# Pick weights laid out by groups of four blocks, and their DMAs issued by SyncE

## The chip, the cores and the metric

One core of one Trainium2 chip runs the program. The metric is device time in microseconds (us), the median of several executions. A profile is one execution, recorded by the hardware; its instructions' times are counted from the span's start.

The engines: TensorE (PE) multiplies matrices, VectorE (DVE), ScalarE (ACT) and GpSimd (POOL) work on tiles, SyncE (SP) does nothing here but issue DMAs. DMAs can also be issued by ScalarE and by GpSimd. SyncE's DMAs are queue q1 of the profile, ScalarE's q10, GpSimd's indirect ones q0; sixteen DMA engines serve all of them.

## The reference

One layer of a decoder trunk, for 512 prompt tokens and 64 sample tokens of width 2048. What matters here is its last part, a mixture of 16384 single-neuron experts (PEER):

```python
q = (xb @ w_q).reshape(PEER_BLOCK, PEER_HEADS, 2, HALF_DIM)
sc = jnp.einsum('thpk,pnk->thpn', q, sub_keys)
v1, i1 = lax.top_k(sc[:, :, 0], PEER_TOPK)
v2, i2 = lax.top_k(sc[:, :, 1], PEER_TOPK)
...                                   # the best 16 of the 256 sums, for each of 8 heads
g = jax.nn.softmax(top, axis=-1)
act = jax.nn.gelu(jnp.einsum('td,thkd->thk', xb, expert_u[eidx])) * g
return jnp.einsum('thk,thkd->td', act, expert_v[eidx])
```

Before it come the modulation (adaLN), an input projection, two recurrent and convolutional head groups and an output projection; after it a last RMSNorm. Everything is in float32.

## The kernel before

**Stages.** Up to about 950 us: modulation, projections, scans. To about 1200 us: the queries and most of the choice of experts. Then two dense stages of about 1000 us each, which the change touches.

The 16384 experts are 128 blocks of 128. The 80 most often picked blocks are computed densely for all 512 prompt tokens; picks that fall in the other 48, and all picks of the sample tokens, are done by gathering single rows of u and v (1 MB per gather of 128 rows), with VectorE multiplying and adding.

- **The u stage** (`for n in range(NU2)`, 160 half blocks): `load(n)` (L892) fetches half a block of u (`raw<-ut`, 512 KB) with SyncE, `conv(n)` splits it into a high part on ScalarE (`xhi`, L908) and a low part on GpSimd (`xlo`, L909), and `u_half` multiplies both with the tokens (`pu`, L1405, three products of float32r for one of float32). After two halves ScalarE applies the gelu (`act`, L1408) and stores the block's activations (`actd<-act`, L1409).
- **The pick weights.** Meanwhile, once the choice is sorted, TensorE makes for each token a 128 x 80 table with the softmax weight of the picked expert, by products of one-hot rows (`gbank`, L1605; the operands come from VectorE, L1591, and ScalarE, L1599). ScalarE copies it out into a tile for 32 tokens (`stg`, L1612), two of which exist. When 32 tokens are done, four stores (`gd<-stg`, L1617, 320 KB each, 20 blocks) are put on a list, `puts`, and `put(2)` issues two of them in each following half.
- **The v stage** (80 steps of 4 columns): `load` fetches pieces of v (`raw<-v`, L897, 256 KB each, four to a step), `conv` splits them, and `v_column` (`pv`, L1425, 12 matmuls a column) adds up the products with the weighted activations. These come in tiles of four blocks (`SG = 4`, 20 tiles): `load_weights` (L1356, `gsb<-gd`, four quarters of 256 KB) and `load_acts` (L1363, `actr<-actd`, two halves of 512 KB) fetch them, `weigh` (L1368, VectorE) multiplies them in place, `halve` splits the product (`ahi`, L1375, ScalarE; `alo`, L1379, VectorE). There is one buffer for gsb and one for actr, so the next tile's loads wait for the product before.

**What sets the order.** From the last query on, the order on every engine is the one in which the code is written (`manual_schedule`), so on each engine's queue an instruction waits behind those written before it. Waits between engines are semaphores that the framework places; every DMA issued by SyncE or ScalarE gets one of eight completion semaphores in turn (DMAHW0 to DMAHW7 in the built program), and waits until the DMA that had it before is complete.

The loads are written ahead of use by `ahead(l, c)`: load up to piece l, split up to piece c. In the u stage there are three raw buffers (`n % 3`), in the v stage five:

```python
ahead(n + 3, n + 2)        # u stage, at the start of half n
...
ahead(n + 3, n + 3)        # v stage, at the start of a step
ahead(n + 8, n + 3)
```

At `E0`, 14 halves before the u stage ends, the remaining stores are issued, the memory of the choice is given free, and the first two weight and activation tiles are loaded into it.

Of the kernel before, what the change touches and what calls it, by code (L numbers as in the profile page):

```python
# [5 lines left out]
F32 = mybir.dt.float32  # L6
# [25 lines left out]
L = 80  # L32
SG = 4
# [3 lines left out]
TC = 32  # L37
NCH = NA // TC
# [43 lines left out]
def build(ctx, tc, A, O, dbg=None):  # L82
    nc = tc.nc
# [6 lines left out]
    dr = ctx.enter_context(tc.tile_pool(name="dr", bufs=1, space=DRAM))  # L90
# [339 lines left out]
    def project(src, nm):  # L430
        his, los = stream_w(src, nm)
        p = pp.tile([128, 2, 512], F32, name=f"pp_{nm}", tag="pp")
        mm3([p[:, 0, :HT], p[:, 1, :HT]], his, los, movs)
        return p
# [183 lines left out]
    for k in range(KD):  # L618
        if k < 2:
            out_half(k, 1)  # L620
            p = p_out[k]
        else:
            p = project(A["w_out"][k], f"o{k}")
# [31 lines left out]
    for q in range(4):  # L655
        modulate(x1, R, None, 3, 4 * q, 4, "h2")
        mm3(pq0, *w_q, movs, range(4 * q, 4 * q + 4))
        t = adap.tile([128, 4, 512], F32, name=f"h2s{q}", tag="wa")
# [41 lines left out]
    identr = rt.tile([128, 128], F32R, name="identr")  # L700
    V.tensor_copy(identr, ident)
    pickd = dr.tile([NA, 2 * NPK], F32, name="pickd")
    gd = dr.tile([NCH, 128, L, TC], F32, name="gd")
    actd = dr.tile([L // SG, 128, SG, NA], F32, name="actd")
    accd = dr.tile([NA, D], F32, name="accd")
    accs = dr.tile([128, D], F32, name="accs")
# [170 lines left out]
    raws, parts, gsb, ahl, acts, pools = {}, {}, {}, {}, {}, {}  # L877
# [6 lines left out]
    def load(n):  # L884
        if n >= len(stream):
            return
        s = stream[n]
        k = n % 3 if n < NU2 + 2 else (n - NU2 - 2) % 5
        pool, b = (ws, 2) if k < 2 else (wx, 1) if k == 2 else (pools["vx"], 2)
        raw = pool.tile([128, 8, 128], F32, name=f"raw{n}", tag="wraw", bufs=b)  # L890
        if s[0] == "U":
            nc.sync.dma_start(raw, A["ut"][bass.ds(block(s[1]), 1), :, 8 * s[2]:8 * s[2] + 8, :].rearrange("o p k c -> p (o k) c"))  # L892
        else:
            _, i, q = s
            r2 = raw.rearrange("p (a k) c -> p a (k c)", a=2)
            for a in range(2):
                nc.sync.dma_start(r2[:, a, :], v3[bass.ds(block(i + a), 1), :, q * VC:(q + 1) * VC].rearrange("o p c -> p (o c)"))  # L897
        raws[n] = raw
# [15 lines left out]
    def ahead(l, c):  # L914
        while at["l"] <= min(l, len(stream) - 1):
            load(at["l"])
            at["l"] += 1
        while at["c"] <= min(c, len(stream) - 1):
            conv(at["c"])
            at["c"] += 1  # L920
# [430 lines left out]
    def load_weights(sg, q):  # L1351

        if q == 0:
            gsb[sg] = ep.tile([128, NCH, SG * TC], F32, name=f"gsb{sg}", tag="gsb", bufs=1)
        c = slice(q * NCH // GP, (q + 1) * NCH // GP)
        nc.scalar.dma_start(gsb[sg][:, c, :], gd[c, :, sg * SG:(sg + 1) * SG, :].rearrange("c p i t -> p c (i t)"))  # L1356

    def load_acts(sg, q):

        if q == 0:  # L1360
            acts[sg] = ep.tile([128, SG, NA], F32, name=f"actr{sg}", tag="actr", bufs=1)
        i = slice(q * SG // AP_, (q + 1) * SG // AP_)
        nc.scalar.dma_start(acts[sg][:, i, :], actd[sg][:, i, :])  # L1363

    def weigh(sg):

# [141 lines left out]
    it, stg, pair, puts = [], {}, {}, []  # L1508
# [99 lines left out]
    def g_out(b, pg):  # L1608
        c, b0 = divmod(b, TC // 4)
        if b0 == 0:  # L1610
            stg[c] = pools["rg"].tile([128, L, TC], F32, name=f"stg{c}", tag="stg", bufs=2)
        S.activation(stg[c][:, :, b0 * 4:b0 * 4 + 4].rearrange("p i t -> p t i"),  # L1612
                     pg[:, :4 * L].rearrange("p (t i) -> p t i", t=4), AF.Copy)
        if b0 == TC // 4 - 1:
            full = stg.pop(c)
            for q in range(0, L, L // 4):
                puts.append(lambda q=q: nc.scalar.dma_start(gd[c][:, q:q + L // 4, :], full[:, q:q + L // 4, :]))  # L1617

    def put(n):
        for f in puts[:n]:  # L1620
            f()
        del puts[:n]
# [20 lines left out]
    for n in range(NU2):  # L1643
        _, i, c = stream[n]
        if n == 0:
            sample_twice()
        if n == 1:
            sample_rows()
        ahead(n + 3, n + 2)
        spare += PIECE if R1 is None else PIECE_G  # L1650
        if R1 is not None:
            put(2)
            g_one(n)
            if not gk:
                g_start()
            elif gm[0] < min(upto(n), gm[1] + PAIRS - 1):
                g_pair(gm[0])
                gm[0] += 2
                spare -= 2.2
            while gm[2] < gm[3]:  # L1660
                g_scale(gm[2])
                gm[2] += 1
            gm[3], gm[4] = gm[4], gm[0]

        even, waits = R2 is not None, False
        while spare > 0 and R2 is None:
            cost = next(steps1 if R1 is None else steps2, "end")
            if cost == "end":
                if R1 is None:
                    R1 = n  # L1670
                else:
                    R2 = n
                break
            if cost is None:
                waits = True
                break
            spare -= cost
        if not even:
            if since is None and ready[0]:
                since = n  # L1680
            if since is not None and n == since + 1:
                fetch_to(RB - 1)
            if since is not None and n > since + 2:
                due_g += RATE[R1 is not None] + (0.7 if waits and spare > 4.5 else 0.0)
            g0 = gu[0]
            gather_to(due_g, ready[0])
            if gu[0] == ready[0] and sorted_[0]:
                fetch_to(gu[0] + 1, ready[0])
            due_g = min(due_g, gu[0] + 1.0)
            spare -= 2.4 * (gu[0] - g0)  # L1690
            if waits:
                spare = min(spare, 3.0)
            G0 = gu[0]
        else:
            gather_to(G0 + (NU + EARLY_V - G0) * (n - R2) // (NU2 - 1 - R2))
        if n == E0:
            assert not pair and not stg
            put(len(puts))
            p2.close()
            epx = ctx.enter_context(ExitStack())  # L1700
            ep = epx.enter_context(tc.tile_pool(name="ep", bufs=1))
        u_half(n, i, c)
        for sg, o in ((0, 1), (1, 7)):
            d = n - E0 - o
            if 0 <= d < 2:
                load_weights(sg, 2 * d)
                load_weights(sg, 2 * d + 1)
            if 2 <= d < 4:
                load_acts(sg, d - 2)
            if d == 5 - sg:  # L1710
                weigh(sg)
            if d == 6 - sg:
                halve(sg, 0)
            if d == 7 - sg:
                halve(sg, 1)
# [39 lines left out]
    for m in range(M):  # L1755
        gi, q, bl, first, final = steps[m]
        n = NU2 + 2 * m
# [6 lines left out]
        for kq in range(KD // VQ):  # L1764
# [7 lines left out]
            if (m, kq) in tplan:  # L1772
                t = len(fin["tok"])
# [168 lines left out]
```

## Time and profile before

| | us |
|---|---|
| median of 3 runs | 3207.52 |
| lowest, highest | 3200.43, 3209.41 |
| the profiled execution | 3200.89 |
| its span, first to last instruction | 3199.1 |
| TensorE busy in it | 3067.4 |
| VectorE, GpSimd, ScalarE busy | 2167.9, 1701.2, 1044.3 |

The issues of the DMAs in question, from the page (count, size of each):

```profile
raw<-ut SPq DMA_DIRECT2D x160, 512.0 KB
raw<-v SPq DMA_DIRECT2D x320, 256.0 KB
actd<-act ACTq DMA_DIRECT2D x80, 256.0 KB
gd<-stg ACTq DMA_DIRECT2D x64, 320.0 KB
gsb<-gd ACTq DMA_DIRECT2D x80, 256.0 KB
actr<-actd ACTq DMA_DIRECT2D x40, 512.0 KB
```

How to read what follows: in a view by stretches, each row gives start and end, the length, the busy time and number of instructions of each engine, the granted TensorE clock (1 is full), the mean busy share of the 16 DMA engines (slightly over 1 is possible at a stretch's edges), and GB/s. Rows of a queue give packets, MB and the time that they took as a share of 16 engines over the stretch. Rows of waits give who waited for whom, the total, how often, and the longest. In the chain of waits each row is a start, a length, and what it was. A `q` after an engine (SPq, ACTq) is its queue of DMA issues.

### The profile page before, as it was taken

Reading aid. Unit: us, or ns where it says so; the run is one execution under the profiler, and the core shown is the slowest. Engines: PE = TensorE matmul, PEld = TensorE weight load, DVE = VectorE, ACT = ScalarE, POOL = GpSimd, SP = SyncE. Lnnn points to the kernel's source line nnn. Section 1 sums busy time; section 2 is a strip of 40 time slices with the busy share of each in tenths; the row PEclk is TensorE's granted clock in tenths of the full one; section 3 lists DMA queues with packets and bytes.
Section 4 is the critical chain, followed back from the end, with each engine's and each line's share of the span. In section 5 each row is a group of like instructions: output and inputs, shape, how many; then the busy total and the mean of one; then the engine's idle time right before and its main releaser. Section 6 shows DMA issues by size and latency. Waiting matters only on the chain.

```text
span 3199.1 us, 46649 instructions
## 1 busy us (share of the span) xinstructions
PE 3067.4 (96%) x17239; PEld 2606.4 (81%) x17239; DVE 2167.9 (68%) x3267; ACT 1044.3 (33%) x1640; POOL 1701.2 (53%) x1001
## 2 busy tenths in 40 slices
PE   6999999999989999999999999998999999899997
PEld 2788888899979998887888788886888878688776
DVE  3455521142245898977898999856777888788755
ACT  3244311122232232232655555542322222121222
POOL 2233333344334235666666666656777677668742
PEclk9999999999989999999999999999999999999998
DMA  9744566633332227899889898989999999899964
GB/s 394 275 139 139 174 218 209 204 121 135 134 117 90 68 82 250 309 314 398 339 309 405 345 410 356 389 288 376 400 386 385 395 329 347 322 399 350 374 206 159
DMA packets 297067, 882.84 MB, mean 276 GB/s; under 512 B 37590, under 2 KB 79446, under 8 KB 245366
## 3 DMA queue, kind: packets, MB, share of 16 engines
q1 hardware_dynamic: 160608, 380.39, 33.8%
q0 software_dynamic: 66336, 413.41, 32.5%
q10 hardware_dynamic: 69888, 86.00, 7.6%
q8 instruction: 136, 2.23, 0.3%
q14 instruction: 99, 0.81, 0.1%
HBM read 879.89 MB, written 66.81 MB: 296 GB/s over the span
## 4 chain that ended last, share of the span: by engine, by line
PE 73%; DMA 11%; POOL 5%; issue 5%; DVE 4%; ACT 1%; SPq 1%; ACTq 0%; POOLq 0%; DVEq 0%
PE pu L1405 20%; PE pv L1425 18%; PE pp_o L140 6%; DMA raw<-v 4%; DMA gsb<-gd 4%; PE pp_c L140 3%; PE pp_s L140 3%; PE qa L140 3%; PE pp_b L140 3%; PE qb L140 3%; POOL xlo L909 3%; PE ada L190 2%; PE pp_x L140 2%; PE pp_y L140 2%; PE gbank L1605 2%
## 5 line engine op out<-in xcount | busy, mean ns | idle before, releaser
L909 POOL TENSOR_TENSOR xlo<-raw,xhi 128x1024 fp32r<-128x1024 f32 x320 | 777.9, 2442 | 420.7 <-ACT xhi L908 408.5
L908 ACT ACTIVATE xhi<-raw 128x1024 fp32r<-128x1024 f32 x320 | 337.5, 1060 | 880.0 <-DMA raw<-v 221.4
L1263 DVE SCALAR_TENSOR_TENSOR u<-u,hT 128x2048 f32<-128x2048 f32 x223 | 503.6, 2283 | 107.4 <-DMA u<-u,rows 88.6
L1290 DVE SCALAR_TENSOR_TENSOR accB<-v,dots,accB 128x2048 f32<-128x2048 f32 x211 | 496.5, 2353 | 106.3 <-DMA v<-v,rows 100.7
L1425 PE MATMUL pv<-ahi,xhi 128*128 128x512 f32 x1280 | 512.0, 400 | 23.8 <-ACT xhi L908 15.7
L1425 PE MATMUL pv<-ahi,xlo 128*128 128x512 f32 x1280 | 510.0, 398 | 11.4 <-POOL xlo L909 11.4
L1405 PE MATMUL pu<-hhi,xhi 128*128 128x512 f32 x1280 | 513.9, 402 | 0.0
L1425 PE MATMUL pv<-alo,xhi 128*128 128x512 f32 x1280 | 506.5, 396 | 0.0
L1405 PE MATMUL pu<-hhi,xlo 128*128 128x512 f32 x1280 | 502.3, 392 | 0.8 <-POOL xlo L909 0.8
L1405 PE MATMUL pu<-hlo,xhi 128*128 128x512 f32 x1280 | 502.9, 393 | 0.0
L1235 POOL DMA_INDIRECT u<-u,rows x223 | 224.3, 1006 | 209.5 <-DVE u L1263 145.0
L1425 PEld LDWEIGHTS pv<-ahi,xhi 128*128 128x128 f32 x1280 | 243.9, 191 | 81.1 <-ACT xhi L908 17.4
L1425 PEld LDWEIGHTS pv<-ahi,xlo 128*128 128x128 f32 x1280 | 243.5, 190 | 72.6 <-POOL xlo L909 16.1
L1425 PEld LDWEIGHTS pv<-alo,xhi 128*128 128x128 f32 x1280 | 244.0, 191 | 55.2
L1405 PEld LDWEIGHTS pu<-hhi,xlo 128*128 128x128 f32 x1280 | 240.8, 188 | 55.6 <-POOL xlo L909 1.5
L1235 POOL DMA_INDIRECT v<-v,rows x223 | 253.5, 1137 | 57.9 <-issue 38.7
L1405 PEld LDWEIGHTS pu<-hhi,xhi 128*128 128x128 f32 x1280 | 241.2, 188 | 49.6 <-issue 0.9
L1405 PEld LDWEIGHTS pu<-hlo,xhi 128*128 128x128 f32 x1280 | 241.2, 188 | 48.3
L1599 ACT ACTIVATE op<-op,it 128x128 f32<-128x128 f32 x512 | 155.4, 389 | 36.7 <-DVE op L1591 34.7
L1605 PEld LDWEIGHTS gbank<-wr,op 128*128 128x128 f32 x1024 | 132.8, 191 | 22.9 <-ACT stg L1612 13.9
L1447 DVE TENSOR_TENSOR acc<-acc,pv 128x512 f32<-128x512 f32 x144 | 97.1, 682 | 67.1 <-PE pv L1425 66.3
L129 POOL TENSOR_TENSOR wlo_o<-raw_o,whi_o 128x1024 fp32r<-128x1024 f32 x32 | 77.5, 2423 | 119.9 <-ACT whi_o L127 119.9
(498 smaller groups left out, 5458.9 us busy)
## 6 DMA issues: line engine op xcount, KB each, us to landing
wa<-w_ada SPq DMA_DIRECT2D x96, 1024.0 KB
raw<-ut SPq DMA_DIRECT2D x160, 512.0 KB
raw<-v SPq DMA_DIRECT2D x320, 256.0 KB
actd<-act ACTq DMA_DIRECT2D x80, 256.0 KB
gd<-stg ACTq DMA_DIRECT2D x64, 320.0 KB
gsb<-gd ACTq DMA_DIRECT2D x80, 256.0 KB
actr<-actd ACTq DMA_DIRECT2D x40, 512.0 KB
raw_o<-w_out SPq DMA_DIRECT2D x32, 512.0 KB
```

Of the source, the lines that this page charges most:

```text
L129: lo_engine(share).tensor_sub(lo, raw, r32(hi))
L140: PE.matmul(o, st, mv[pick](k), start=first, stop=last)
L908: S.activation(hi, raw, AF.Copy)
L909: G.tensor_sub(lo, raw, r32(hi))
L1235: G.indirect_dma_start(out=out, out_offset=None, in_=src, in_offset=bass.IndirectOffsetOnAxis(ap=idx, axis=0), bounds_check=NE * 128 - 1, ...
L1263: V.scalar_tensor_tensor(r, r, 1.0, st["h"], op0=ALU.mult, op1=ALU.mult, accum_out=dots[i][:, j:j + 1])
L1290: V.scalar_tensor_tensor(st["a"], r, dots[i][:, j:j + 1], st["a"], op0=ALU.mult, op1=ALU.add)
L1405: PE.matmul(pu, st[:, kk, :], movA[mv](k), start=k == 0 and a == 0, stop=k == KD - 1 and a == 2)
L1425: PE.matmul(pv, st, mv, start=first and j == 0 and a == 0, stop=last and not end and j == SG - 1 and a == 2)
L1447: V.tensor_add(ak, ak, pv)
L1599: S.activation(ops[:, j0 + j, :], ops[:, j0 + j, :], AF.Copy, scale=it[2][:, b * 4 + j:b * 4 + j + 1])
L1605: PE.matmul(pg[:, j * L:(j + 1) * L], ops[:, j0 + j, :], wr[:, j0 + j, :], start=True, stop=True)
```

## The change

Three edits. **The layout of `gd`**, the pick weights in memory, goes from chunks of 32 tokens outermost, `[chunk, partition, block, token]`, to groups of four blocks outermost, `[group, partition, chunk, block of the group, token]`. A quarter of a gsb tile is then 4 x 4 x 32 numbers in a row for each partition, where it was four runs of 4 x 32; a store of 20 blocks is five runs of 4 x 32 for each partition, where it was one of 20 x 32. The bytes and the number of DMAs stay. **The issuer** of the stores of pick weights and of the loads of pick weights and activations becomes SyncE. ScalarE keeps the stores of activations. **Raw u** is written up to five half blocks ahead: a second call follows the first, with nothing more to split.

```diff
-    gd = dr.tile([NCH, 128, L, TC], F32, name="gd")
+    gd = dr.tile([L // SG, 128, NCH, SG, TC], F32, name="gd")
...
-        nc.scalar.dma_start(gsb[sg][:, c, :], gd[c, :, sg * SG:(sg + 1) * SG, :].rearrange("c p i t -> p c (i t)"))
+        nc.sync.dma_start(gsb[sg][:, c, :], gd[sg][:, c].rearrange("p c i t -> p c (i t)"))
...
-        nc.scalar.dma_start(acts[sg][:, i, :], actd[sg][:, i, :])
+        nc.sync.dma_start(acts[sg][:, i, :], actd[sg][:, i, :])
...
-                puts.append(lambda q=q: nc.scalar.dma_start(gd[c][:, q:q + L // 4, :], full[:, q:q + L // 4, :]))
+                puts.append(lambda q=q: nc.sync.dma_start(
+                    gd[q // SG:(q + L // 4) // SG, :, c].rearrange("s p i t -> p s (i t)"),
+                    full[:, q:q + L // 4, :].rearrange("p (s i) t -> p s (i t)", i=SG)))
...
         ahead(n + 3, n + 2)
+        ahead(n + 5, n + 2)
```

What this does to the order on the engines, at the places of which the prediction speaks (numbers are part of the names; `x2` stands for two such rows).

ScalarE in the v stage, before: the splits of raw v, with the loads of weights and activations between them.

```order
L908 ACTIVATE xhi_21459<-raw_21279 128x1024
L1356 DMA gsb_21536<-gd 128x4x128
L908 ACTIVATE xhi_21551<-raw_21288 128x1024
L908 ACTIVATE xhi_21555<-raw_21375 128x1024
L1375 ACTIVATE ahi_21577<-actr_21315 128x2048
L1356 DMA gsb_21536<-gd 128x4x128 x3
L908 ACTIVATE xhi_21641<-raw_21384 128x1024
L908 ACTIVATE xhi_21645<-raw_21463 128x1024
L1363 DMA actr_21690<-actd 128x1024 x2
L908 ACTIVATE xhi_21742<-raw_21472 128x1024
```

With the change the six DMA rows are gone from ScalarE here, and the splits follow each other. They stand on SyncE, here for the next tile, behind the raw v loads of the same step (TENSOR_LOAD and ISA read and use the block's number):

```order
L897 DMA raw_21943<-v 128x512
L881 TENSOR_LOAD blk
L897 ISA
L897 DMA raw_21943<-v 128x512
L1356 DMA gsb_21911<-gd 128x512 x3
L881 TENSOR_LOAD blk
L897 ISA
L897 DMA raw_22024<-v 128x512
```

SyncE had nothing but raw loads there before; a load of the next step now waits behind the three quarters.

SyncE in the u stage, with the change: the stores of one chunk of 32 tokens between raw u loads.

```order
L892 DMA raw_15365<-ut 128x1024
L1617 DMA gd<-stg_14986 128x5x128 x2
L881 TENSOR_LOAD blk
L892 ISA
L892 DMA raw_15430<-ut 128x1024
L1617 DMA gd<-stg_14986 128x5x128 x2
L881 TENSOR_LOAD blk
L892 ISA
L892 DMA raw_15483<-ut 128x1024
```

Before, only the raw rows stood here, and the four stores stood on ScalarE behind splits of raw u.

## The prediction

> **What bounds the kernel now.** I read the page first: busy shares, DMA row, queues, chain.
>
> ```profile
> PE 3067.4 (96%) x17239; PEld 2606.4 (81%) x17239; DVE 2167.9 (68%) x3267; ACT 1044.3 (33%) x1640; POOL 1701.2 (53%) x1001
> DMA  9744566633332227899889898989999999899964
> q1 hardware_dynamic: 160608, 380.39, 33.8%
> q0 software_dynamic: 66336, 413.41, 32.5%
> q10 hardware_dynamic: 69888, 86.00, 7.6%
> PE 73%; DMA 11%; POOL 5%; issue 5%; DVE 4%; ACT 1%; SPq 1%; ACTq 0%; POOLq 0%; DVEq 0%
> PE pu L1405 20%; PE pv L1425 18%; PE pp_o L140 6%; DMA raw<-v 4%; DMA gsb<-gd 4%; PE pp_c L140 3%; PE pp_s L140 3%; PE qa L140 3%; PE pp_b L140 3%; PE qb L140 3%; POOL xlo L909 3%; PE ada L190 2%; PE pp_x L140 2%; PE pp_y L140 2%; PE gbank L1605 2%
> ```
>
> TensorE is the bound almost everywhere. The DMA engines are nearly full from slice 15 on, the two dense stages, and only there do DMAs (raw v, and the pick weights gsb) enter the chain. Which queue is whose follows from sizes: q0 the gathers, q1 SyncE's, q10 ScalarE's. Next the view by stretches, for what TensorE loses.
>
> ```profile
> core 0: us, PE busy (x) PEld busy (x) DVE busy (x) ACT busy (x) POOL busy (x), PEclk, DMA share, GB/s
> 2200.00:3040.00 840.00, 804.81 (x3417) 648.33 (x3416) 672.84 (x379) 193.64 (x185) 598.31 (x362) 0.98 0.97 368
> 2280.00:2520.00 240.00, 240.00 (x1043) 195.40 (x1042) 184.71 (x111) 54.48 (x49) 170.53 (x104) 1.00 1.01 388
> 2200.00:2240.00 40.00, 30.09 (x120) 23.18 (x119) 25.49 (x12) 11.91 (x14) 25.37 (x16) 0.87 0.93 363
> 2560.00:2600.00 40.00, 35.10 (x133) 27.06 (x132) 29.56 (x18) 8.15 (x7) 26.15 (x15) 0.87 0.95 358
> 2760.00:2800.00 40.00, 28.45 (x103) 21.48 (x104) 34.78 (x16) 9.13 (x9) 29.43 (x18) 0.83 0.96 341
> 2960.00:3000.00 40.00, 33.30 (x135) 25.86 (x134) 29.93 (x18) 8.89 (x8) 23.92 (x15) 0.95 1.00 371
> ```
>
> The undisturbed stretch has 1043 matmuls in 240 us: 0.230 us each, 174 in 40 us. The v stage, 840 us, would hold 3651 at that pace and has 3417: 234 missing, **54 us**. The four short stretches lack 54, 41, 71 and 39, together 205, or 47 of the 54. Their clock is below 1: a stall also buys some microseconds at half clock. The chain of waits, in order of time, shows what each stall hangs on.
>
> ```profile
> 2533.78 30.96 DMA gsb<-gd
> 2564.86 0.33 SPq L897
> 2565.70 11.13 DMA raw<-v
> 2578.07 2.39 POOL xlo L909
> 2580.51 136.63 PE pv L1425 x580
> ...
> 2718.14 29.98 DMA gsb<-gd
> ...
> 2826.14 28.09 DMA gsb<-gd
> ```
>
> A quarter of a gsb tile (256 KB) takes 28 to 31 us; when it lands, SyncE issues a raw v load, 11 us later that lands, is split, and TensorE resumes. Yet raw v and gsb share no data. In the built program each load issued by SyncE or ScalarE waits for the completion semaphore of an earlier one, eight semaphores serving both queues in turn; so a slow gsb holds a raw load back. The waits of SyncE's and ScalarE's queues from 2240 to 3040 us say how much:
>
> ```profile
> SPq L897 <- POOL xlo L909: 187.7, 72, 7.2
> SPq L897 <- DMA raw<-v: 161.0, 55, 13.1
> SPq L897 <- DMA gsb<-gd: 105.3, 13, 18.4
> SPq L897 <- DMA actr<-actd: 30.6, 13, 4.5
> ...
> ACT xhi L908 <- DMA raw<-v: 212.5, 38, 16.3
> ...
> ACT xhi L908 <- DMA actr<-actd: 31.9, 5, 8.6
> ACT xhi L908 <- DVE actr L1368: 29.0, 3, 11.3
> ACT xhi L908 <- DMA gsb<-gd: 25.8, 3, 8.6
> ```
>
> The last three rows are ScalarE standing in front of its own gsb and actr issues while the next split (L908) is queued behind.
>
> **The change part by part.** *Layout of gd.* A quarter tile was 512 runs of 512 B and becomes 128 runs of 2 KB; a store was 128 runs of 2560 B and becomes 640 of 512 B. Prices, each from a stretch in which one size makes up nearly all of a queue (gsb on q10 from 2624.7 to 2635.3; raw v on q1 from 2242 to 2264; gd stores on q10 from 1755.9 to 1762):
>
> ```profile
> q10 hardware_dynamic: 2112, 1.05, 35.9%
> ...
> q1 hardware_dynamic: 1710, 3.11, 38.1%
> ...
> q10 hardware_dynamic: 98, 0.25, 10.2%
> ```
>
> 35.9% of 16 engines x 10.6 us over 2112 packets is 28.8 ns for 512 B; likewise 78 ns for 2 KB and 102 ns for 2560 B. Loads: 80 x 512 x 28.8 ns / 16 = 74 us of all engines' time become 80 x 128 x 78 / 16 = 50, a saving of 24, some 21 of it in the v stage. Stores: 64 x 128 x 102 / 16 = 52 us become 64 x 640 x 28.8 / 16 = 74, a cost of 22 in the u stage. No row shows 512 B written to memory; from below it is the read's 28.8 ns, from above a whole packet of the old store, 102 ns, which would cost 209 us; I take the read's, since 2 KB read and 2560 B written cost alike per byte (0.038 and 0.040 ns).
>
> The Trainium skill ("DMA: Bandwidth & Descriptors", Specifications) puts the smallest transfer at line rate at 512 B, by which neither side of the new layout would change the engines' time and both terms, -21 and +22, would be nothing. The rows disagree: 512 B in 28.8 ns is a third fewer bytes per ns than 2 KB in 78, so the measurement decides.
>
> *What that is worth in the v stage.* Its DMA work is 0.97 x 840 = 815 us and falls to 794; TensorE needs 3417 x 0.230 = 786. So the stage cannot end earlier than about 794 by DMA: at most 46 us of gain, unless the gathers fill less of it. From below: if the engines stay idle for the 25 us that they are now, the gain is the 21 us saved. Between lies the order of issue. All streams now stand in one queue, complete in nearly the order of issue, and a semaphore used eight issues earlier is then mostly free, so the 105 + 31 us of SyncE's waits on gsb and actr should shrink to waits on plain backlog. I take **33 us**: the stage at 807, a DMA share of 0.984, between the 0.97 of the whole and the 1.01 that the undisturbed stretch held while TensorE lost nothing.
>
> *ScalarE rid of 184 issues.* From the rows of these tiles:
>
> ```profile
> L1356 ACTq DMA_DIRECT2D gsb<-gd x80: 367/408/12334, 2153.0 to 3009.8; - x80
> L1617 ACTq DMA_DIRECT2D gd<-stg x64: 326/442/1412, 1564.6 to 2138.0; - x64
> ```
>
> About 0.4 us each, 75 us, on an engine that is busy 33%: nothing by itself (its idle time hides them; were it the bound, 75 us); its 87 us of waits above are part of the 33. SyncE takes the issues over and does no other work. But now SyncE stands before a gsb load until the product before it (DVE, L1368) is done, with raw loads behind; those have 3 steps of 48 matmuls, 11 us each, before they are split, and the longest such wait on ScalarE was 11.3: nothing (without that lead, up to 11 us a tile).
>
> *The u stage.* Stores enter SyncE's queue between raw u loads. Raw n+5 reuses the buffer that split n+2 has just left, so issuing it five ahead puts it before the stores, and it still goes out when the buffer is free, as before: nothing, where three ahead would have left it behind two stores. What is new is one ring.
>
> ```profile
> 1560.00:2120.00 560.00, 552.66 (x2865) 465.96 (x2864) 506.82 (x636) 323.05 (x706) 350.20 (x237) 1.00 0.92 367
> 1680.00:1800.00 120.00, 114.26 (x588) 94.49 (x586) 107.87 (x147) 66.41 (x145) 73.47 (x51) 1.00 1.00 411
> ...
> ACT xhi L908 <- DMA raw<-ut: 28.7, 15, 4.8
> PEld gbank L1605 <- ACT stg L1612: 12.6, 13, 3.6
> ```
>
> (The last two: waits from 1560 to 1800.) The engines have room on average: 0.92 x 560 + 22 = 537 of 560. But in the first 240 us the split already waits for raw u, 15 times, and TensorE then waits for ScalarE behind it. Two stores are 16 shares per engine of 5 x 28.8 ns; with a gather's 8 KB (at most 0.33 us, by q0's row of the page: 32.5% of 16 x 3199 us over 413.41 MB) between each two, they occupy the ring for 7.6 us, by which the next raw u may land later. Lower end nothing; upper end 7.6 us in each of the 240 / 36 = 6.7 chunks of that window, 51 us (36 us: 16 chunks from 1565 to 2138). I take one shift, **7 us**: raw u is released by GpSimd's split, not by TensorE, so a TensorE that has fallen 7 us behind finds the next loads in time. The move to v, at 2200, is in the 33.
>
> **Sum:** -33 + 7 = -26. The profiled execution took 3200.89 us (span 3199.1), 6.6 below the median of 3207.52 whose runs spread over 9; against the median, 3207.5 - 26 = **3181 us**.
>
> **Rivals.** (1) *All stalls go*: 54 back, no price in u: 3153. For it: four stalls hang on the same wait. Against: 794 us of DMA work. (2) *DMA time is the bound*: 21 saved in v, 22 paid in u, and idle engines as now: about 3207. For it: share 1.00 in both stages' worst stretches. Against: 45 us idle in u. (3) *Slower, by stores ahead of raw u*: in SyncE's ring the delay returns with every chunk, 51 - 33 = +18, 3225. It decides once the delays in u add up to more than 33 us, that is, when over 4 of the 16 chunks cost 7.6 us each. For it: raw u has no slack there now; against: one shift makes slack. (4) *Slower, by the share of the queue*: in v three queues become two; from 2240 on SyncE's one ring must carry what took two, and with a gather always waiting, each 2 KB of weights or raw v costs 0.33 + 0.08 us. It decides if raw v then lands as late as it did behind gsb: nothing is gained in v, u's 7 stay: 3214. Against it: the gathers wait for row buffers. The Trainium skill ("DMA: Bandwidth & Descriptors", Queues, rings and completion order) has each engine go round the queues packet by packet, by which moving two streams into one queue costs them a turn, as in (4); the gsb quarters of 28 to 31 us on a queue of their own agree with waiting for turns.
>
> The change does what it says: the built order has all 184 DMAs on SyncE.
>
> **Chances.** Forecast 0.52 (its own range 3165 to 3198), rival 1 0.14, rival 2 0.16, rival 3 0.11, rival 4 0.07. What a measurement here tells from no change is 0.3%, 9.6 us: faster below 3198, slower above 3217. Faster: 0.52 x 0.95 + 0.14 + a fifth of rival 2 = 0.66; same: the rest of these and half of rival 4, 0.19; slower: rival 3 and half of rival 4, 0.15. Range 3148 to 3215: it leaves out the lowest of rival 1 and most of rival 3.
>
> **What would show it.** Right: matmuls from 2200 to 3040 up to some 3560, no gsb in the chain, SyncE's waits on gsb under 30 us, ScalarE's on actr and gsb gone; u stage longer by under 10 us. Wrong: raw<-ut waits of the split far above 40 us and the v stage starting 20 us later or more (rival 3); raw<-v waits above 212 us with as many matmuls lost (rival 4); q1's 512 B packets well above 29 ns (the store's price); DMA share at 1.00 throughout v with 230 matmuls missing still (rival 2).

## The result, and the profile after

The changed kernel takes **3250.01 us** (median of 4 runs, 3246.95 to 3259.81), the kernel before 3208.47 beside it: a ratio of 1.0136, with a 95% interval of 1.011 to 1.0161. It is slower by 1.4%, where 0.8% faster was forecast, and outside the range.

The profiled execution of the changed kernel took 3248.33 us. Its page, with the rows that answer to those shown of before:

```profile
PE 3075.5 (95%) x17239; PEld 2615.7 (81%) x17239; DVE 2160.2 (67%) x3267; ACT 1041.4 (32%) x1640; POOL 1705.6 (53%) x1001
q1 hardware_dynamic: 219872, 443.31, 39.3%
q10 hardware_dynamic: 12672, 23.07, 1.9%
PE 69%; DMA 17%; DVE 5%; issue 4%; POOL 3%; ACT 1%; SPq 0%; POOLq 0%; DVEq 0%; ACTq 0%
PE pu L1405 19%; PE pv L1425 16%; DMA raw<-v 7%; PE pp_o L140 6%; DMA raw<-ut 6%; PE pp_c L140 3%; PE pp_s L140 3%; PE qa L140 3%; PE pp_b L140 3%; PE qb L140 3%; PE pp_x L140 2%; PE pp_y L140 2%; PE ada L190 2%; PE gbank L1605 2%; POOL xlo L909 2%
```

The gsb load is gone from the chain's list, as forecast, but DMA has 17% of the chain (11% before), and raw u, which was not in the list at all, has 6%. In what follows the u stage is the time from the first `pu` product to the first `pv` product, the v stage from the first to the last `pv` product, both from the trace. Before, they are 1025.4 and 960.6 us; in the changed kernel 1072.0 and 961.2. So **u lost 47 us and v gained nothing.** The view by stretches, of the changed kernel and then of the kernel before (the last row of each is the same piece of v, counted from 30 us ahead of its first product):

```profile
1560.00:2120.00 560.00, 514.97 (x2615) 435.00 (x2614) 480.25 (x611) 291.90 (x650) 324.52 (x221) 0.95 0.90 344
2200.00:3040.00 840.00, 812.29 (x3467) 656.78 (x3466) 656.22 (x374) 197.56 (x189) 600.70 (x361) 0.98 0.96 371
2231.00:3111.00 880.00, 844.76 (x3593) 682.28 (x3592) 694.98 (x397) 206.25 (x196) 620.46 (x373) 0.98 0.94 363
```

```profile
2184.00:3064.00 880.00, 844.01 (x3586) 679.98 (x3585) 708.60 (x398) 205.16 (x195) 616.93 (x371) 0.98 0.96 363
```

While the pick weights are stored, TensorE issues 2615 matmuls where it issued 2865, and the DMA engines are less busy than before (0.90 against 0.92): on the average of this stretch they are not the bound. In v the DMA share falls from 0.96 to 0.94, some 18 us of DMA work (16 by the packets' own times) where 21 was forecast, and the matmuls stay about the same (3593 against 3586).

**Where u went.** Waits from 1560 to 2160 us in the changed kernel, and then the same four in the kernel before:

```profile
POOL xlo L909 <- ACT xhi L908: 197.1, 57, 13.3
ACT xhi L908 <- DMA raw<-ut: 83.1, 13, 14.9
PEld gbank L1605 <- ACT stg L1612: 48.6, 9, 14.0
PE gbank L1605 <- ACT stg L1612: 45.0, 8, 13.5
```

```profile
POOL xlo L909 <- ACT xhi L908: 38.0, 13, 8.5
ACT xhi L908 <- DMA raw<-ut: 32.6, 17, 4.8
PEld gbank L1605 <- ACT stg L1612: 13.1, 14, 3.6
PE gbank L1605 <- ACT stg L1612: 7.1, 9, 3.2
```

TensorE does not wait for raw u. It waits for ScalarE to copy out the bank of the one-hot products (`stg`, L1612), and ScalarE stands ahead of that copy at the split of a half block that TensorE needs only two halves later. One such place in ScalarE's timeline (start, length, what, and in brackets the idle time before it):

```profile
1718.84 0.33 ACTq L1409 DMA_DIRECT2D actd<-act  x1
1731.88 1.06 ACT L908 ACTIVATE xhi<-raw 128x1024 fp32r<-128x1024 f32 x1 [13.07 <-DMA raw<-ut]
1732.84 0.70 ACT L1612 ACTIVATE stg<-gbank 128x320 f32<-128x320 f32 x1
```

That raw u load had been issued at 1704.55, behind two stores, as SyncE's timeline shows:

```profile
1697.27 1.04 SPq L1617 DMA_DIRECT2D gd<-stg  x2
1704.55 0.59 SPq L892 DMA_DIRECT2D raw<-ut  x1
1705.19 19.25 SPq L1617 DMA_DIRECT2D gd<-stg  x2
```

The chain of waits has it, with others like it:

```profile
1580.82 26.19 DMA raw<-ut
...
1704.55 27.25 DMA raw<-ut
...
1911.12 24.95 DMA raw<-ut
```

Why a 512 KB load took 27 us is told by the queues from 1704.5 to 1728 (packets, MB, share of 16 engines):

```profile
q0 software_dynamic: 1183, 8.64, 87.7%
q1 hardware_dynamic: 1187, 0.60, 8.4%
```

SyncE's queue moved 1187 packets, nearly all of 512 B (1170 by size in the trace, 27 ns each), and the gathers' queue 1183 (1055 of 8 KB, 309 ns each): about one for one. The order agrees: up to 1727 us, 1197 times a 512 B packet begins in the 6 ns before an 8 KB packet ends, where some 290 would be chance, and there is no such peak of 512 B packets behind one another. **Every piece of 512 B (a run of bytes in a row) took a turn of its own, against 8 KB of a gather.** The two stores of 1697.27 are 80 pieces on each engine, 80 x (0.309 + 0.027) = 27 us, and the raw load queued behind them comes after that: none of its 4 KB packets moves before 1728. By the Trainium skill ("DMA: Bandwidth & Descriptors", Queues, rings and completion order) an engine drains a packet of typically 9 to 17 descriptors before it turns to the next queue; by estimate 80 pieces would then be at most 9 turns, some 5 us by the durations above if a gather's turn is one 8 KB. The rows disagree for these stores.

**Where v went.** Waits at the product of weights and activations (L1368) in the stretch 2231 to 3111 of the changed kernel:

```profile
DVE actr L1368 <- DMA raw<-v: 45.4, 6, 16.0
DVE actr L1368 <- DMA actr<-actd: 31.3, 5, 11.8
DVE actr L1368 <- issue: 9.6, 2, 6.2
```

VectorE stands 86 us before this product; before it was 13 us in the same piece of v. The product does not read raw v; its operands now come in one queue with raw v. From issue to landing actr takes 18.2 us at the median (9.5 before), gsb 10.7 (16.6 before). ScalarE's splits wait less for raw v (144 us, 221 before): part of the stall has moved from the raw loads to the weighted activations.

### The profile page after: what moved, and what is told of

The parts are those of the page before. It is cut to its first block, busy times and chain, and to the rows that moved or that the text cites. A ratio compares the mean times of both kernels' runs of the same rounds, so it can differ in the third digit from the quotient of the medians.

```text
span 3246.5 us, 46716 instructions
## 1 busy us (share of the span) xinstructions
PE 3075.5 (95%) x17239; PEld 2615.7 (81%) x17239; DVE 2160.2 (67%) x3267; ACT 1041.4 (32%) x1640; POOL 1705.6 (53%) x1001
## 4 chain that ended last, share of the span: by engine, by line
PE 69%; DMA 17%; DVE 5%; issue 4%; POOL 3%; ACT 1%; SPq 0%; POOLq 0%; DVEq 0%; ACTq 0%
PE pu L1405 19%; PE pv L1425 16%; DMA raw<-v 7%; PE pp_o L140 6%; DMA raw<-ut 6%; PE pp_c L140 3%; PE pp_s L140 3%; PE qa L140 3%; PE pp_b L140 3%; PE qb L140 3%; PE pp_x L140 2%; PE pp_y L140 2%; PE ada L190 2%; PE gbank L1605 2%; POOL xlo L909 2%
## 5 line engine op out<-in xcount | busy, mean ns | idle before, releaser
L1605 PE MATMUL gbank<-wr,op 128*128 128x80 f32 x1024 | 135.2, 276 | 45.2 <-ACT stg L1612 45.2
```

Of the source, the lines that this page charges most:

```text
L1605: PE.matmul(pg[:, j * L:(j + 1) * L], ops[:, j0 + j, :], wr[:, j0 + j, :], start=True, stop=True)
```

## The experiments

All runs, with u and v against the kernel before (1025.4 and 960.6), and TensorE's waits for the copy of the bank (`PE gbank <- ACT stg`, 1540 to 2240 us). The u and v columns come from one profile each, and a profiled execution can lie well off its kernel's median: 19 us above it for the stores on ScalarE, 12 below for SyncE and five ahead alone, 11 below for the groups of 8, 9 below for the activations on ScalarE. Kernels whose v stage is the same as the change's gave 954 to 965 there, and the change and the run with the loads on ScalarE, the same program up to half block 146, need 995 and 1005 us of u to get there: less than 10 us is not read from these columns alone. Where the expectations say ring, they mean a queue.

| run | median us | ratio to before (95%) | u | v | gbank waits |
|---|---|---|---|---|---|
| the change | 3250.01 | 1.0136 (1.011 to 1.0161) | +47 | 961 | 45 |
| layout alone | 3278.98 | 1.0239 (1.0198 to 1.0279) | +92 | 937 | 80 |
| SyncE and five ahead alone | 3205.55 | 1.0009 (0.9991 to 1.0026) | +4 | 952 | 10 |
| stores on ScalarE | 3294.89 | 1.0268 (1.0225 to 1.0311) | +104 | 965 | 84 |
| without five ahead | 3265.95 | 1.0176 (1.0137 to 1.0215) | +64 | 962 | 55 |
| loads on ScalarE | 3239.68 | 1.0103 (1.0079 to 1.0126) | +60 | 938 | 50 |
| activations on ScalarE | 3241.69 | 1.0115 (1.0094 to 1.0137) | +50 | 945 | 43 |
| groups of 8 | 3238.14 | 1.0107 (1.0084 to 1.013) | +33 | 952 | 32 |
| groups of 16 | 3204.82 | 1.0004 (0.9985 to 1.0024) | +3 | 959 | 10 |
| old layout, activations on ScalarE | 3230.39 | 1.0062 (1.0038 to 1.0087) | +10 | 976 | 12 |
| one store a half | 3268.64 | 1.0177 (1.0135 to 1.0219) | +68 | 954 | 58 |
| gathers in two halves | 3260.89 | 1.0153 (1.0118 to 1.0188) | +57 | 961 | 32 |
| stores in the gathers' queue | 3195.47 | 0.9957 (0.9937 to 0.9976) | +14 | 940 | 12 |
| fourth raw buffer | 3214.56 | 1.0029 (1.001 to 1.0048) | +26 | 943 | 28 |
| fourth buffer, gathers' queue | 3187.06 | 0.9936 (0.9914 to 0.9958) | +10 | 937 | 10 |
| before, gathers in two halves | 3252.19 | 1.0137 (1.0106 to 1.0168) | +44 | 969 | 4 |
| gathers' queue, no five | 3192.23 | 0.996 (0.9944 to 0.9975) | +15 | 940 | 11 |

Apart from the two runs with divided gathers, which have a price of their own, u's loss and TensorE's waits at the bank go together row by row.

### One part at a time

*The layout alone:* the change with all 184 DMAs issued by ScalarE as before, and without the second call of `ahead` in u.

```diff
-        nc.sync.dma_start(gsb[sg][:, c, :], gd[sg][:, c].rearrange("p c i t -> p c (i t)"))
+        nc.scalar.dma_start(gsb[sg][:, c, :], gd[sg][:, c].rearrange("p c i t -> p c (i t)"))
...
-        ahead(n + 5, n + 2)
```

> The new layout of gd alone; issuers and lead of raw u as before. In the changed kernel the whole loss is in the u stage (its last product starts 46.8 us later), the v stage takes the same 961 us, and a raw u load that stood behind four stores landed 26 us after its issue where 8 to 9 us were usual. Theory A (turns): the 512 B packets of a store each wait for one 8 KB packet of a gather, and on SyncE's queue raw u waits behind them. Then here raw u lands in 8 to 9 us again, u's loss is at most 15 us, and the stores, on a queue of their own, land later than the 12 us of before. Theory B (order of SyncE's issues, whatever the packets' size): u's loss 0. Theory C (the layout's writes are dear in themselves): u's loss 30 us or more. For v: if merging the queues ate the gain of the wide loads (S), v gets 20 to 35 us shorter here; if v is bound by the amount of DMA work (W), by at most 10 us.

*SyncE and five ahead alone:* the kernel before with `nc.sync` in the three places and the second call, in the old layout.

> The issues on SyncE and raw u five ahead, with the old layout: stores of 2560 B, loads of pick weights of 512 B. A: four stores are 32 packets per engine instead of 160, raw u lands at most 8 us later, u's loss under 12 us. B: u's loss is that of the change, about 47 us. C: u's loss 0. In v the 512 B packets are on the loads' side: by A they hold raw v up in SyncE's queue, v is longer than before by 20 us or more; by S as well; by W it stays within 10 us of before.

*Stores on ScalarE:* the change with `nc.scalar` for the stores only.

> The change with the stores of pick weights issued by ScalarE again (new layout, loads on SyncE, raw u five ahead). A: raw u in 8 to 9 us, u's loss at most 15 us, as with the layout alone. B: u's loss 0. C: u's loss 30 us or more. v as in the change, 961 us within 8, so the total is 3200 to 3220 by A.

*Without five ahead:* the change without the second call.

> The change without the second call, raw u written three ahead. A: two raw u loads that went ahead of the stores now stand behind them, so u loses more than the 47 us of the change, by 10 to 60 us. If the lead does nothing: the same as the change within 8 us.

The layout loses u's time and the order of issue does not: in the old layout SyncE's stores cost 4 us, and theory B is out. With the new layout's stores on ScalarE the loss is larger, 92 and 104 us, where theory A had 15 at most. Raw u did land in time there, as A has it (90th percentile from issue to landing 8.4 and 8.8 us, 18 in the changed kernel); what A left out is the issue. The stores' row of the run with the layout alone (durations of the issue itself: shortest, median, longest, ns), and one of its waits from 1560 to 2160 us (2.5 us in the kernel before):

```profile
L1617 ACTq DMA_DIRECT2D gd<-stg x64: 366/629/14430, 1567.8 to 2229.7; - x64
...
ACT stg L1612 <- issue: 99.2, 16, 18.8
```

An issue that lasted at most 1412 ns before now holds ScalarE up to 14.4 us, and the copies of the bank stand behind it. That it lasts until the queue has room for the 640 pieces is an inference, with which the runs with fewer pieces below agree. On SyncE it is held as long (18.8 us at most in the changed kernel), but there only raw loads wait. So moving the stores to SyncE was worth some 57 us by the profiles (1129 against 1072) and 45 by the medians, given the layout. Five ahead was worth 18 us of u (16 by the medians, with intervals that overlap). Theory C had a loss of 30 or more in these runs, but its ground, that writes of 512 B are dear by themselves, is refuted by the 27 ns above.

In v the layout alone gains 23 us, and the change with its stores put back on ScalarE nothing: what the layout gains is lost where the loads share SyncE's queue. That is theory S, and theory W (the amount of DMA work) is out. But S, like A, also had v 20 us longer with the old layout in SyncE's queue, and there it is 952, not longer than before. So the one queue is not slow by itself. With both loads on SyncE the layout makes no difference that these profiles tell: v is 952 to 959 with loads of 512 B pieces (this run, and the groups of 8 and 16 below) and 954 to 965 with 2 KB, and VectorE stands 66 to 91 us at L1368 in all of them. With the loads on ScalarE it does: 961 before, 937 to 943 with 2 KB. Why the gain needs a queue of its own was not taken further apart than in the next two runs.

### Who issues the loads in v

```diff
-        nc.sync.dma_start(gsb[sg][:, c, :], gd[sg][:, c].rearrange("p c i t -> p c (i t)"))
+        nc.scalar.dma_start(gsb[sg][:, c, :], gd[sg][:, c].rearrange("p c i t -> p c (i t)"))
...
-        nc.sync.dma_start(acts[sg][:, i, :], actd[sg][:, i, :])
+        nc.scalar.dma_start(acts[sg][:, i, :], actd[sg][:, i, :])
```

> The change with the loads of weights and activations back on ScalarE; the stores and raw u five ahead stay with SyncE. Theory Q (the one ring of SyncE took back what the layout gave in v): v stage 935 to 945 us as with the layout alone (937), VectorE's waits for actr and raw v at L1368 under 15 us (86 in the changed kernel), u stage as in the changed kernel, 47 us longer; whole kernel 3220 to 3235. Rival V (the v stage is bound by the DMA engines whoever issues; the 937 was only the later state of the gathers after a u stage of 1117 us): v stage 955 or more, kernel 3245 to 3255.

With only the second of these two edits:

> The change with only the loads of activations (actr) back on ScalarE; weights (gsb) stay with SyncE. Theory Q1 (what comes too late in SyncE's ring is actr, behind raw v, and VectorE with its row sums stands at L1368 for it): VectorE's waits there fall from 86 to under 20 us and the v stage to 935 to 947; kernel 3222 to 3238. Rival Q2 (any load more in SyncE's ring holds raw v back, gsb as much as actr): v stage halfway, 949 or more, with raw v waits of the splits as before, kernel above 3238.

Waits at L1368 from 2250 to 3130 us, with both loads on ScalarE, and then with the activations alone:

```profile
DVE actr L1368 <- DMA actr<-actd: 4.8, 1, 4.8
DVE actr L1368 <- DMA raw<-v: 3.1, 1, 3.1
```

```profile
DVE actr L1368 <- DMA gsb<-gd: 16.1, 3, 10.2
DVE actr L1368 <- DMA actr<-actd: 2.1, 1, 2.1
```

Theory Q holds: v is 938 and the 86 us at L1368 are 8. The kernel's time missed its range by 5 us, since u was 60 longer here, and that of the next run by 4. With the activations alone v is 945 and VectorE's waits are 18 us, as Q1 has it; but one profile does not tell 945 from Q2's 949, and the kernel's 3241.69 lies on Q2's side. So most of v's loss seems to be actr behind raw v in one queue, and some of it gsb; the shares are not settled. By the Trainium skill ("DMA: Bandwidth & Descriptors", Issuing engines are not separate DMA queues) issuing on several engines saves no more than the time to issue; here, with 2 KB pieces, the queue that two loads go into is worth 23 us of v.

The same in the old layout (`nc.sync` for stores and gsb, `nc.scalar` for actr, five ahead):

> The layout from before the change; stores and loads of weights issued by SyncE, loads of activations left on ScalarE, raw u five ahead. Theory Q1 (in v the late one in SyncE's ring is actr): VectorE's waits at L1368 for actr fall from the 62 us of the run with the queue alone to under 15, v stage 938 to 946 (952 there, 961 before); u stage +2 to +6; kernel 3185 to 3196, ratio 0.993 to 0.998. Rival: the gsb quarters of 512 runs hold raw v in the same ring, v 950 or more, ratio 0.999 to 1.003.

This missed on the other side: v is 976, longer than before. The waits of SyncE's queue from 2250 to 3130 us:

```profile
SPq L1356 <- DMA actr<-actd: 72.5, 9, 13.4
SPq L897 <- DMA gsb<-gd: 61.1, 25, 9.7
SPq L1356 <- DMA gsb<-gd: 39.9, 11, 9.4
```

SyncE waits 72 us in front of gsb loads for actr, which ScalarE issues and with which gsb shares no data; gsb lands after 20.4 us (11.9 with all on SyncE). With actr on ScalarE and the new layout the same wait is 44 us, and v is good all the same. Which part of this is shared semaphores and which the 512 B pieces was not separated.

### Pieces, turns and bytes

*Groups of 8 and of 16 blocks in memory*, stored 16 blocks at a time, issued and loaded by SyncE: the bytes of a chunk stay, its pieces per DMA engine are 80 of 1 KB or 40 of 2 KB, where the change has 160 of 512 B and the old layout 32 of 2.5 KB.

```diff
-    gd = dr.tile([L // SG, 128, NCH, SG, TC], F32, name="gd")
+    gd = dr.tile([L // 8, 128, NCH, 8, TC], F32, name="gd")
...
-            for q in range(0, L, L // 4):
+            for q in range(0, L, 16):
```

> The change with pick weights laid out by groups of eight blocks, stored 16 blocks at a time: a store is 256 pieces of 1 KB where it was 640 of 512 B, the bytes of a chunk are the same (80 pieces per DMA engine and chunk where there were 160); a quarter of a gsb tile is read as 512 runs of 512 B, as before the change. Theory T (every piece takes a turn of its own beside a gather's 8 KB, 0.32 us): 80 turns are 26 us and fit into a chunk's 36 to 40: u stage longer than before the change by 20 us or less, SyncE held by a store's issue for 10 us at most (18.8 in the changed kernel), v stage 948 to 956. Rival P (the price is of stores that are cut into places far apart at all, or of stores in SyncE's ring ahead of raw u): u longer by 30 us or more.

> The same with groups of sixteen blocks: a store of 16 blocks is 128 runs of 2 KB, 40 pieces per DMA engine and chunk (32 before the change, at 2.5 KB). Theory T: 13 us of turns a chunk, u stage within 10 us of before the change, as with the old layout issued by SyncE (+4); v stage 948 to 956; kernel 3195 to 3212. Rival P: u longer by 20 us or more still, kernel above 3215.

16 blocks cost 3 us as theory T has it, and the half of rival P that blames any store in SyncE's queue ahead of raw u is out. Its other half (stores cut into places far apart) is not tried by this run, whose stores are one piece for each partition; the stores in the gathers' queue below, cut as in the change, speak against it. For 8 blocks T's number failed, 33 us for at most 20, where P had 30 or more. A sum made after these two runs accounts for it: T had left out that raw u's own packets take turns in the same queue: 45 of 4 KB per engine and chunk, 45 x (0.309 + 0.159) = 21 us. With them a chunk asks SyncE's queue for 34, 37, 49 and 75 us (32, 40, 80 and 160 pieces), against the 36 us that a chunk lasts, if a gather is always waiting. The losses, 4, 3, 33 and 47 us over 16 chunks, begin where the demand clearly passes the chunk; they are smaller than the excess, since a gather is not always waiting. The issue's hold grows with the number of pieces in a store: with 256 it lasts 1487 ns at most.

```profile
L1617 SPq DMA_DIRECT2D gd<-stg x80: 359/452/1487, 1576.9 to 2178.7; - x80
```

*One store a half* (`put(1)` for `put(2)`):

> The change with one store put into each half block of u instead of two. Theory T (total turns: 160 pieces per engine and chunk beside raw u's 45 packets are 75 us of turns in a chunk of 36, if a gather always waits): as many turns, so u still 40 us or more longer than before. Rival B (it is the burst of two stores that raw u's three buffers cannot bridge): u longer by 25 us or less, kernel below 3232.

T holds, and the burst of two is not the cause. This run loses more than the change, as the two `stg` tiles now come free late (`ACT stg <- DMA gd<-stg` 49.7 us). An issue of 640 pieces here lasts 3810 ns at most on SyncE, so the hold follows not a store's own pieces alone but also those that still stand ahead of it.

*Gathers in two halves*, in the change and as a control in the kernel before:

```diff
-            take(held[j][0], A["u"], rows_i[i][:, j:j + 1])
+            for h in range(2):
+                G.indirect_dma_start(out=held[j][0][:, h * 1024:(h + 1) * 1024], out_offset=None, in_=A["u"],
+                                     in_offset=bass.IndirectOffsetOnAxis(ap=rows_i[i][:, j:j + 1], axis=0),
+                                     element_offset=h * 1024, bounds_check=NE * 128 - 1, oob_is_err=False)
```

> The change with every gather of rows of u in two, 4 KB of each row at a time, the bytes the same: a turn is half as long. Theory T: 160 pieces x (0.155 + 0.027) + 45 raw packets x (0.155 + 0.156) = 43 us a chunk where it is 75; raw u's 90th percentile from issue to landing falls from 18 us towards 12, u stage longer than before by 5 to 30 (47 in the change). Rival D (small pieces are slow by themselves, whatever goes beside them): u longer by 42 to 60, landing as in the change.

> The kernel before with only the gathers of rows of u in two halves of 4 KB a row: 223 gathers become 446, at 1.0 us of GpSimd each, bytes unchanged. If the 15 us lost by the same edit ahead of half 60, and more behind it, are GpSimd's, u is longer than before by 20 to 45 us here too; then of the 57 us lost with the change most were this price, and the pieces cost 12 to 35. If u is longer by under 10 us, halving the turn did not help the change at all (theory T short of a reason).

Against the changed kernel raw u's 90th percentile from issue to landing falls from 18.4 to 13.8 us, as T expects of turns half as long, but u's loss does not fall below 30; read alone that speaks for D. The control accounts for most of it: the same edit costs 44 us without the new layout, by twice as many gathers on GpSimd. The pieces then cost 57 - 44 = 13 us, where they cost 47 beside whole rows. It is not clean, since a u stage that GpSimd holds up leaves room in which late loads cost nothing.

*Stores in the gathers' queue:* `nc.gpsimd` for the stores, loads of weights and activations on ScalarE.

```diff
-                puts.append(lambda q=q: nc.sync.dma_start(
+                puts.append(lambda q=q: nc.gpsimd.dma_start(
```

> The new layout with the stores issued by GpSimd, into the queue of the gathers themselves, loads on ScalarE, raw u five ahead. Theory T: in one ring stores and gathers take no turns with each other; raw u meets at most one of them per packet, its 90th percentile falls to 10 us or less. What it costs is GpSimd's time for the 640 pieces of a store, which no row shows: at 1 us for 128 rows, as for a gather, 5 us a store, 20 a chunk on an engine that is busy 23 of 36; then GpSimd's split of raw u is late and u is longer by 10 to 90 all the same. v stage 938. Rival D: raw u lands as late as in the change.

> Stores in the gathers' queue, loads on ScalarE, without raw u five ahead. Both theories: no store stands in SyncE's queue, so the fourth and fifth load are issued when their buffer is free either way; u as with five ahead (1039 within 6 us), kernel 3190 to 3203. Rival: u longer by 10 us or more, so five ahead is worth something by itself.

This beats the kernel before, by 0.4%, and all of that is v's gain: u is still 14 us longer. Raw u lands as before the change (90th percentile 8.9 us, longest 11.8), and the fear for GpSimd was wrong: an issue takes 0.9 us, not 5.

```profile
L1617 POOL DMA_DIRECT2D gd<-stg x64: 872/916/932, 1579.9 to 2161.1; - x64
```

The reason is only in part the one expected. The page's queue row has 72480 packets for the gathers' queue, 6144 more than before, or 96 for each store; by size in the trace 80 of them hold 4 KB, at 172 ns. GpSimd's queue moved eight pieces of 512 B in one packet, SyncE's one by one:

```profile
q0 software_dynamic: 72480, 434.39, 34.4%
```

So a store was 5 packets per engine where it was 40, and this run does not tell whether one queue or few packets did it. Five ahead does nothing here (u 1040 with and without), as nothing stands in SyncE's queue ahead of raw u.

### Raw u's lead

A fourth buffer for raw u from half 72 to 144, paid for by one pair fewer of one-hot tables; DMAs unchanged. First with the stores on SyncE, then in the gathers' queue; loads on ScalarE in both.

```diff
-PAIRS = 8
+PAIRS = 6
...
+        if A0 <= n < A1:
+            k = (n - A0) % 4
+            pool, b = (ws, 2) if k < 2 else (wx, 1) if k == 2 else (pools["rg"], 1)
...
+        if A0 + 3 <= n + 6 <= A1 + 2:
+            ahead(n + 6, n + 2)
```

> The change with loads of weights and activations on ScalarE (as in the run with the loads on ScalarE) and a fourth buffer for raw u from half block 72 to 144, loaded six ahead; its memory is taken from the one-hot tables (three pairs of them instead of four). The DMAs of u are the same. Theory L (raw u lands later than its lead; ScalarE then stands at the split and TensorE waits for the gbank copy behind it): the lead grows from 19 to 25 us, over the 90th percentile of 18 to 20; PE's waits gbank <- stg fall from 50 to under 20 us and u is longer than before the change by 5 to 25 (60 in that run, 47 in the change). Rival E (the DMA engines have no more to give beside 512 B pieces): u longer by 40 or more, landing later still. v stage 938.

> The same fourth buffer with the stores issued by GpSimd into the gathers' queue. Raw u lands within 9 us there already, far within 19; theory L: the fourth buffer changes nothing against that run (u 1039, 14 longer than before; v 940), kernel 3188 to 3200. Rival G (what is left there is GpSimd, late with its split by the issue of the stores, which a deeper raw buffer bridges): u shorter by 5 us or more, kernel 3180 to 3190.

With the stores on SyncE u's loss falls from 60 to 26 us, while raw u lands as late as without (90th percentile 18.1 us). So late raw u against too short a lead is the larger part, and rival E is out. It is not all: TensorE still waits 28 us at the bank (under 20 expected), now partly because the `stg` tiles wait for their stores. Waits from 1540 to 2240 us (line numbers are five higher here):

```profile
PE gbank L1610 <- ACT stg L1617: 28.2, 8, 8.6
ACT stg L1617 <- DMA gd<-stg: 19.4, 5, 6.8
```

With the stores in the gathers' queue the kernel takes **3187.06 us, 0.9936 (0.9914 to 0.9958)** of the kernel before: the lowest median of all, with an interval that overlaps that of the same without the buffer. Against that run u is 4 us shorter, between what L and G expected and below what one profile tells.

## Why the prediction was wrong

**The DMA work: right.** 512 B written takes 27 ns where 28.8 was taken, and v's DMA work fell by 16 to 18 us where 21 was said. The 78 ns for 2 KB were too low, since that row of 1710 packets counts 190 of 4 B; by size it is 87 ns in that stretch.

**The u stage: the step that failed.** The prediction put it so: "Two stores are 16 shares per engine of 5 x 28.8 ns", and, with a gather's 8 KB between each two, "they occupy the ring for 7.6 us". The turn was right and was priced, 0.33 us for a measured 0.309, but it was given to each partition's row of five pieces. Each piece takes it: 80 turns, 27 us, not 7.6. From that size the one shift of 7 us that was taken for the whole stage fell too: 27 us is beyond the 19 that three raw buffers bridge (three halves of 6.4 us), so the delay came back, and u lost 47. The 47 us lie inside the term's bounds (0 to 51), near the upper end, but that is luck: the upper end was reached with the wrong price. And the place where TensorE pays, `gbank <- stg`, stood in the prediction's own fence with 12.6 us: "TensorE then waits for ScalarE behind it".

**The v stage: the layout's saving was there, the 33 us were not.** The prediction had at most 46 us and at least the 21 that the layout saves; the runs with the loads on ScalarE gain 18 to 24. But the 33 were taken for the one queue's sake ("All streams now stand in one queue"), and in the one queue nothing of the layout's gain was left: 961 us, as before. SyncE's wait for gsb did shrink (34 us from 114 in the same piece of v), but VectorE's at L1368 grew from 13 to 86: the prediction asked whether SyncE would stand before the product and not whether the product would stand before its loads. Rival 4 had this mechanism, in raw v where it came in actr.

**ScalarE rid of 184 issues: nothing, said the prediction**, at 0.4 us each. With these stores an issue is not 0.4 us: left on ScalarE they cost 57 us of u more (45 by the medians). The quoted row of before had the hint in its third number, 12334 ns for a gsb load of 512 pieces, where only the median was used.

**Raw u five ahead: right.** It is worth some 16 to 18 us where stores stand on SyncE, and nothing that shows where they do not.

**What would show it.** From 2200 to 3040 there are 3467 matmuls, not 3560 (v begins at 2261 here, so that stretch is no longer all v). The raw<-ut waits are 83 us, far above 40, and v begins 47 us later: these two are the signs named for rival 3, which had a chance of 0.11 and the price of 51 - 33. Its mechanism is what happened in u; with v's gain gone as in rival 4 the sum is 47 + 0, and 3207.5 + 47 = 3254 by the prediction's own base.

**Left open.** Why the wide loads gain in v from ScalarE's queue and not from SyncE's, where the narrow ones lose nothing. Why the old layout with only actr on ScalarE lost 15 us in v. How much of the gain in the gathers' queue is the queue and how much the larger packets, and why u is still 10 to 15 us longer there. The fourth buffer was not tried with all four pairs of one-hot tables, for want of memory.

## What to carry to other kernels

Count a DMA's packets before its bytes: beside the stream of 8 KB gathers here, each 512 B piece in SyncE's queue cost a turn of 0.31 us on top of its own 0.027, and everything behind it in its queue paid for all of them. When a layout is turned over to make loads longer, see where the stores become short and what is queued behind them; here the shorter stores had to go where nothing urgent follows. And a wait taken from one stream by putting it into another's queue can come back at a later reader, here VectorE: look at who reads what the moved loads bring.

## What the runs showed that was not expected

- SyncE's queue moved 512 B pieces one to a turn (1187 packets against 1183 of the gathers in 23.5 us); GpSimd's moved the same store in packets of 4 KB, 172 ns each.
- Issuing a DMA of 640 pieces held the issuing engine up to 14.4 us on ScalarE and 18.8 on SyncE, 3.8 us at most on SyncE where the stores were a half block apart; one of 256 pieces 1.5 us at most, and on GpSimd one of 640 took 0.9 us.
- Late data can cost time through an engine's order without being needed yet: raw u landed a median of 23.5 us ahead of its products in the changed kernel (16.6 before), and still cost 47 us, through a copy that stood behind its split.
